# LN0's normalized rows kept in DRAM, and the residual added by VectorE instead of by products with the identity

## The chip, the core and the metric

The kernel runs on one core of a Trainium2 chip. The metric is device time in microseconds for one execution, the median of several runs; lower is better. The core has TensorE (PE, with PEld for its weight loads), VectorE (DVE), ScalarE (ACT), GpSimd (POOL), and SyncE (SP), which here only issues transfers. Sixteen DMA engines move the data of all queues; SP's queue carries the weights, POOL's queue the small tables, gathers and scatters.

## The reference

512 tokens of width 1024 pass one layer of an encoder. The parts that matter here:

```python
h = layer_norm(x, ln0_g, ln0_b)                     # "LN0": rows normalized, then gain and offset
mix = merged @ w_out                                # merged = sigmoid(ga)*out_a + sigmoid(gb)*out_b
h = layer_norm(DN_ALPHA * h + mix, ln1_g, ln1_b)    # the residual h is LN0's output
ffn = routed_experts(h, ...)                        # top 4 of 32 experts per token, chosen by h @ w_router
h = layer_norm(DN_ALPHA * h + ffn, ln2_g, ln2_b)
```

`out_a` and `out_b` are a windowed and a dense attention, each followed by its own branch projection. An expert has three 1024 x 1024 float32 matrices (gate, up, down), 12 MB in all, 32 experts.

## The kernel before

All instructions of an engine run in the order in which the code issues them (a manual schedule), and a tile name with `bufs=n` is a ring of n buffers: the next tile of that name waits until the oldest one's readers are done.

Tokens are four tiles of 128 (t = 0 to 3). At the start `acc` holds x, is normalized in place (mean and variance only), and is transposed; gain and offset go on during the transposition. The result stands as `hTH` + `hTL`, two fp32r parts of LN0's output with the width on the partitions. After that `acc` is used for the attention outputs (`oAB`), which are split into `qs` and `kk` (L702 to L708).

The stretch around the change, in order:

- **Branch projections** (L712 to L728), four rounds `cc`. A round makes four results in PSUM tiles `s` (3 buffers), 12 matmuls each: two for branch A from `qs`, two for branch B from `kk`. VectorE multiplies each by its gate (L721), adds the pairs (L724), and ScalarE and VectorE split the sum, divided by alpha, into two parts `M` (L726, L727). VectorE also makes the low part of the weights that come next (L94).
- **Router constants** (L732 to L744). POOL's queue loads LN1's gain and offset into the ring `P` (4 buffers of 128 x 512, used by the attention until then), then the router's weights `wr` (tile `tab`) and its bias `cb`, then `order` (tile `PT`) and the experts' biases. TensorE multiplies `wr` by LN1's offset (L743), eight products that stand in its order ahead of the output projection.
- **Residual** (L749 to L754). 64 products of 128 x 128 blocks of `hTH` and `hTL` with the identity put LN0's output, turned back to rows, into the eight PSUM tiles `oo` of the output projection.
- **Output projection** `mix` (L756), adding onto them: k = 0 to 3 for all tiles, then k = 4 to 7 tile by tile. After each tile `norm` (L764) takes statistics of the PSUM tiles (L300, L301), and ScalarE writes the normalized rows `z` (L768). Two tiles later `z_turn` transposes them, ScalarE copies the result to `kp` (L779), and `route` (L781) multiplies by `wr` (L784) and picks the four experts. POOL makes h (`affine`, L792) from `z` for the gathers.
- **Order of the experts** (L916 to L958): the counts per expert give `turns` and `turnI`. From expert 1 on SP reads the expert's number from `turnI` (L219) before it can issue a load (L237).

Expert 0's twelve chunks of 1 MB need no number. They are loaded ahead into slots, of which seven are opened at L822 in the space that `hTH`, `hTL`, `kk` and `qs` leave.

Of the kernel before, what the change touches and what calls it, by code (L numbers as in the profile page):

```python
# [10 lines left out]
F32 = mybir.dt.float32  # L11
# [4 lines left out]
AF = mybir.ActivationFunctionType  # L16
OP = mybir.AluOpType
# [4 lines left out]
DM = 1024  # L22
T = 512
NT = T // 128
KT = DM // 128
# [3 lines left out]
ALPHA = 2.0 ** 0.25  # L29
SCALE = HD ** -0.5  # L30
SLOPES = [2.0 ** -(h + 1) for h in range(NH)]
LN_EPS = 1e-5
# [86 lines left out]
def hybrid_attention_moe(ctx: ExitStack, tc: tile.TileContext, x, ln0_g, ln0_b, w_in, a_sink, b_q_norm, b_k_norm,  # L119
                         w_branch_a, w_branch_b, w_out, ln1_g, ln1_b, w_router, b_router, w_gate, b_gate,  # L120
                         w_up, b_up, w_down, b_down, ln2_g, ln2_b, consts, dist, order, rope, out):
    nc = tc.nc
# [6 lines left out]
    def pool(name, **kw):  # L129
        p = tc.alloc_tile_pool(name=name, bufs=1, reuse_waits="tile", **kw)  # L130
        opened.append(p)
        return p

    def close(*pools):
        for p in pools:
            opened.remove(p)
            p.release()

    ctx.callback(lambda: close(*opened[::-1]))
    dram = ctx.enter_context(tc.tile_pool(name="dram", bufs=1, space=DRAM))  # L140
    keep = pool("keep")
    wp = pool("wp")
    hd = pool("hd")
# [16 lines left out]
    def mm3(o, ah, al, bh, bl, start, stop, **kw):  # L160

        for i, (a, b) in enumerate(((ah, bh), (ah, bl), (al, bh))):
            nc.tensor.matmul(o, a, b, start=start and i == 0, stop=stop and i == 2, **kw)  # L163

    def run(g):
        for _ in g:
            pass
# [4 lines left out]
    acc = keep.tile([128, NT, DM], F32, name="acc")  # L172
# [35 lines left out]
    for c in range(4):  # L208
        v = w_out.rearrange("(k p) c -> p k c", p=128)[:, 2 * c:2 * c + 2]
# [80 lines left out]
    def ln_stats(rows_, eps=LN_EPS, pool=keep):  # L290

        return ln_scale(row_stats(rows_, pool), eps, pool)

    def row_stats(rows_, pool=keep):
        n = len(rows_)
        bs = pool.tile([128, n, 2, 6], F32, name="bst", bufs=2 if pool is keep else 1)
        mv = pool.tile([128, n, 2], F32, name="mv", bufs=2 if pool is keep else 1)
        for t, src in enumerate(rows_):
            for i in range(2):
                nc.vector.bn_stats(bs[:, t, i], src[i])  # L300
            nc.vector.bn_aggr(mv[:, t], bs[:, t])  # L301
        return mv

    def ln_scale(mv, eps=LN_EPS, pool=keep):
        n = mv.shape[1]
        r = pool.tile([128, 2, n], F32, name="rstd", bufs=2 if pool is keep else 1)
        rstd_of(r[:, 0], mv[:, :, 1], 1.0, eps)
        nc.vector.scalar_tensor_tensor(r[:, 1], mv[:, :, 0], -1.0, r[:, 0], op0=OP.mult, op1=OP.mult)
        return [(r[:, 0, t:t + 1], r[:, 1, t:t + 1]) for t in range(n)]
# [6 lines left out]
    def two(a):  # L316
        return [a[:, :512], a[:, 512:]]


    hTH = h1.tile([128, KT, T], F32R, name="hTH")  # L320
    hTL = h1.tile([128, KT, T], F32R, name="hTL")
    identr = h1.tile([128, 128], F32R, name="identr")
# [3 lines left out]
    for i in range(2):  # L326
        for t, (r, nmr) in enumerate(stats):
            z = two(acc[:, t])[i]
            if t % 2:
                nc.vector.tensor_scalar(z, z, r, nmr, op0=OP.mult, op1=OP.add)  # L330
            else:
                nc.scalar.activation(z, z, AF.Identity, bias=nmr, scale=r)
    p = ps.tile([128, 32], F32, name="pp", bufs=2)
    nc.tensor.transpose(p, rows, ident[:32, :32])
    nc.vector.tensor_copy(cols, p.rearrange("p (a b) -> p a b", b=8))
# [26 lines left out]
    def proj_k(halves, done, tag, bufs):  # L362
        p = [ps.tile([128, 2, 256], F32, name=tag, bufs=bufs) for _ in range(2)]
        for i, half in enumerate(halves):
            wh, wl = st.get(half)
            for t in (0, 2, 1, 3):
                s = slice(t * 128, t * 128 + 128)
                for k in range(4):
                    q = 4 * i + k
                    o = p[t // 2][:, t % 2]  # L370
                    for j, (a, b) in enumerate(((hTH, wh), (hTL, wh), (hTH, wl))):
                        nc.tensor.matmul(o, a[:, q, s], b[:, k], start=t % 2 == 0 and q == 0 and j == 0,
                                         stop=q == KT - 1 and j == 2, skip_group_check=True)
                if i:
                    done(t, p[t // 2][:, t % 2])
                yield
# [135 lines left out]
    w = {}  # L512
# [27 lines left out]
    bias = [hd.tile([128, T], F32, name=f"gb{h}") for h in range(NH)]  # L540
# [29 lines left out]
    for i in range(2):  # L570
        nc.vector.tensor_tensor(tab[i][:, :, 0], ropes[:, :, 0], qkn[:, i:i + 1].to_broadcast([128, NT, HD]), op=OP.mult)
        for a in range(2):
            sw = qkn[:, i].rearrange("p (h a d) -> p h a d", a=2, d=16)[:, :, 1 - a]
            for t in range(NT):
                nc.vector.tensor_tensor(tab[i][:, t, 1].rearrange("p (h a d) -> p h a d", a=2, d=16)[:, :, a],
                                        ropes[:, t, 1].rearrange("p (h a d) -> p h a d", a=2, d=16)[:, :, a],
                                        sw, op=OP.mult)
# [27 lines left out]
    def q_done(c):  # L605
        def done(t, p):
            s = slice(c * 256, c * 256 + 256)
            nc.scalar.activation(rq[t].rearrange("p n d -> p (n d)")[:, s], p, AF.Copy)
            if c == 0:
                sq[t] = hd.tile([128, T], F32, name="P", bufs=4)  # L610
            nc.scalar.activation(sq[t][:, s], p, AF.Square)
            if c:
                nc.vector.reduce_sum(rs[:, t, 0:8], sq[t].rearrange("p (n d) -> p n d", d=HD), AX.X)
        return done
# [43 lines left out]
    g0, g1 = proj_k(h_bq[0], q_done(0), "s", 3), proj_k(h_bq[1], q_done(1), "pp", 2)  # L658
# [44 lines left out]
    for i, n in enumerate(("qs", "kk")):  # L703
        d = h1.tile([128, 4, DM], F32R, name=n).rearrange("p a (b c) -> p (a b) c", c=T)
# [3 lines left out]
        o_hl.append((d[:, 0:4], d[:, 4:8]))  # L708
    run(gates_b)
    gv = {}  # L710
    M = []
    for cc in range(4):  # L712
        for i, g in enumerate((gA, gB)):
            wh, wl = st.get(h_br[2 * cc + i])
            for c in (2 * cc, 2 * cc + 1):
                nc.scalar.activation(g[c], g[c], AF.Sigmoid)
                p = ps.tile([128, T], F32, name="s", bufs=3)
                s = slice(c % 2 * 128, c % 2 * 128 + 128)
                for k in range(4):
                    mm3(p, wh[:, k, s], wl[:, k, s], o_hl[i][0][:, k], o_hl[i][1][:, k], k == 0, k == 3)  # L720
                nc.vector.tensor_tensor(g[c], p, g[c], op=OP.mult)  # L721
        for c in (2 * cc, 2 * cc + 1):
            m = hd.tile([128, T], F32, name="f", bufs=2)
            nc.vector.tensor_tensor(m, gA[c], gB[c], op=OP.add)  # L724
            h, l = hd.tile([128, T], F32R, name=f"ga{c}"), hd.tile([128, T], F32R, name=f"gb{c}")
            nc.scalar.activation(h, m, AF.Copy, scale=1.0 / ALPHA)  # L726
            nc.vector.scalar_tensor_tensor(l, m, 1.0 / ALPHA, h.bitcast(F32), op0=OP.mult, op1=OP.subtract)  # L727
            M.append((h, l))  # L728

    for n, v in (("g1", ln1_g), ("b1", ln1_b)):  # L732
        for i in range(2):
            gv[n, i] = hd.tile([128, T], F32, name="P", bufs=4)
            nc.gpsimd.dma_start(gv[n, i], v[:, i * 512:i * 512 + 512].to_broadcast([128, 512]))
    wr = hd.tile([128, 2, KT, NE], F32, name="tab")
    nc.gpsimd.dma_start(wr[:, 0], w_router[0].rearrange("(k p) e -> p k e", p=128))
    nc.vector.tensor_tensor(wr[:, 1], wr[:, 0], cols[:, 2][:, :, None].to_broadcast([128, KT, NE]), op=OP.mult)
# [7 lines left out]
    iota_e = con[:, C_IE:C_IE + NE]  # L746
    h1d = dram.tile([T, DM], F32, name="h1d")

    def residual(t, o):  # L749
        s = slice(t * 128, t * 128 + 128)  # L750
        for k in range(KT):
            for h in (hTH, hTL):
                nc.tensor.matmul(o[k // 4][:, k % 4 * 128:k % 4 * 128 + 128], h[:, k, s], identr,
                                 start=k % 4 == 0 and h is hTH, stop=False, skip_group_check=True)  # L754

    def mix(t, o, k, w, last):  # L756
        for i in range(2):
            s = slice(i * 512, i * 512 + 512)
            mm3(o[i], *(m[:, t * 128:t * 128 + 128] for m in M[k]), w[0][:, 0, s], w[1][:, 0, s], False, last,
                skip_group_check=True)  # L760

    z = {}

    def norm(t, o):  # L764
        (r, nmr), = ln_stats([o], LN_EPS / ALPHA ** 2)
        z[t] = [hd.tile([128, T], F32, name=("ga", "gb")[i] + str(t)) for i in range(2)]
        for i in range(2):
            nc.scalar.activation(z[t][i], o[i], AF.Identity, bias=nmr, scale=r)  # L768

    zt = {}  # L770

# [43 lines left out]

    oo = [[ps.tile([128, T], F32, name=n, bufs=b) for _ in range(2)] for n, b in (("pp", 2), ("pt", 2), ("s", 3))]
    oo.append([ps.tile([128, T], F32, name=n, bufs=b) for n, b in (("s", 3), ("o", 1))])
    for t in range(NT):
        residual(t, oo[t])
    close(h1)  # L820
    rp = pool("rp", side="right")
    st.slots(rp, 7)  # L822
# [52 lines left out]
    for k in range(4):  # L875
        w = st.get(h_wo[k])
# [87 lines left out]
    for k in range(KT):  # L964
        f = mp.tile([128, T], F32, name="rT")[:, k % 4 * 128:k % 4 * 128 + 128]
        g, b = (cols1[:, c, k:k + 1] for c in range(2))
        h, l = (d[:, k] for d in XT[0])
# [335 lines left out]
    for e in range(NE):  # L1303
        f = e + 1
        if f < NE:
            gates_of(f, {1: [blocks] if f == 10 else [], 5: [lambda: a_turn(e, 0)], 6: [lambda: a_turn(e, 1)]})
            at = {}
            n = min(2, NE - 3 - f)
# [74 lines left out]
    with tc.If(n_over > 0):  # L1383
# [8 lines left out]
        with tc.For_i(0, n_over, 1) as i:  # L1392
# [31 lines left out]
            def fetch(w):  # L1424
                def get(j):
                    raw = mp.tile([128, DM], F32, name="raw", bufs=3)
                    nc.sync.dma_start(raw, w[0, ds(e, 1)].rearrange("a (p j) f -> (a p) j f", j=8)[:, j])
                    h, l = hl((1, DM))()
                    split_to(h[:, 0], l[:, 0], raw)
                    return h, l  # L1430
                return get
# [12 lines left out]
            o = products(range(8), AT["o"], None, None, "d", {}, fetch(w_down))  # L1444
# [61 lines left out]
```

## Time and profile before

| | us |
|---|---|
| median of 3 runs (1462.32 to 1465.82) | 1463.74 |
| the profiled execution, its own time | 1464.82 |
| its span in the trace, first to last instruction | 1463.0 |

| engine | busy us | share of the span |
|---|---|---|
| PE | 1385.2 | 95% |
| PEld | 925.6 | 63% |
| DVE | 885.3 | 61% |
| ACT | 718.2 | 49% |
| POOL | 226.9 | 16% |

Busy shares are means over stages with different limits, so the page's slices and the windows by stage say more than they do. Times in the rows count from the span's start. In a row of waits, "A <- B" says that A stood idle until B was done.

### The profile page before, as it was taken

The numbers are of one execution on the slowest core, as the hardware profiler recorded it, in microseconds if no ns is written. First come the engines' busy times: TensorE is split into PE (matmuls) and PEld (weight loads), VectorE is DVE, ScalarE is ACT, GpSimd is POOL, SyncE is SP. The second block draws the span as 40 slices with busy tenths as digits, with TensorE's granted clock in tenths as the row PEclk, the third lists the DMA queues.
The fourth block names the chain that finished last, engine by engine and source line by source line (L and its number), as shares of the span: only waits on it lengthen the run. The fifth ranks groups of instructions, "written<-read, shape, count | busy, mean of one in ns | idle before, by whom it ended". The sixth has DMA issues, their size and how long they took to land.

```text
span 1463.0 us, 19181 instructions
## 1 busy us (share of the span) xinstructions
PE 1385.2 (95%) x6837; PEld 925.6 (63%) x6837; DVE 885.3 (61%) x1384; ACT 718.2 (49%) x1016; POOL 226.9 (16%) x264
## 2 busy tenths in 40 slices
PE   5999999999879999999999999999999999999973
PEld 4778977888755547466574755747556486567521
DVE  5666676563674537466584664846547388577355
ACT  5454567533353526355463553735546276566301
POOL 0000200102451110112101121011210103130002
PEclk9999999999889999999999999999999999999987
DMA  6462211327279999999999999999999999999981
GB/s 228 155 230 67 80 37 36 108 94 282 75 260 356 414 423 423 423 399 418 424 422 420 423 423 420 415 415 416 414 417 414 414 408 425 410 409 423 388 365 63
DMA packets 90645, 469.55 MB, mean 321 GB/s; under 512 B 10369, under 2 KB 28977, under 8 KB 42416
## 3 DMA queue, kind: packets, MB, share of 16 engines
q1 hardware_dynamic: 80160, 439.54, 74.0%
q0 software_dynamic: 10384, 28.73, 5.2%
q8 instruction: 55, 0.90, 0.2%
q14 instruction: 46, 0.38, 0.1%
HBM read 451.71 MB, written 24.64 MB: 326 GB/s over the span
## 4 chain that ended last, share of the span: by engine, by line
PE 28%; DMA 22%; issue 17%; DVE 3%; POOL 2%; ACT 1%; POOLq 0%; SPq 0%; DVEq 0%
DMA raw<-in_w_up_dram 6%; DMA raw<-in_w_down_dram 6%; PE d L163 6%; DMA raw<-in_w_gate_dram 6%; PE g L163 5%; PE u L163 5%; PE u L1100 4%; PE g L1100 3%; DMA xg<-h1d,tokI 3%; PE d L1100 3%; POOL hots L801 1%; PE t L1023 1%; DVE raw L1361 1%; PE t L1162 1%; DMA Y<-y,dstI 1%
## 5 line engine op out<-in xcount | busy, mean ns | idle before, releaser
L94 DVE TENSOR_TENSOR wl<-raw,wh 128x1024 fp32r<-128x1024 f32 x428 | 514.8, 1229 | 126.2 <-ACT wh L93 120.2
L93 ACT ACTIVATE wh<-raw 128x1024 fp32r<-128x1024 f32 x428 | 444.8, 1057 | 173.1 <-PE d L163 66.8
L1015 POOL DMA_INDIRECT xg<-h1d,tokI x31 | 46.2, 1491 | 710.3 <-PE t L1162 322.5
L158 DVE TENSOR_TENSOR atl<-t,ath 128x512 fp32r<-128x512 f32 x32 | 22.0, 690 | 153.8 <-ACT ath L157 153.8
L1100 PE MATMUL g<-raw,xth 128*64 128x512 f32 x480 | 112.5, 601 | 0.0
L1100 PE MATMUL d<-raw,ath 128*64 128x512 f32 x480 | 110.4, 599 | 0.0
L1100 PE MATMUL u<-raw,xth 128*64 128x512 f32 x480 | 109.8, 599 | 0.0
L163 PE MATMUL d<-wh,ath 128*128 128x512 f32 x256 | 105.2, 411 | 2.2 <-ACT wh L93 2.2
L163 PE MATMUL d<-wl,ath 128*128 128x512 f32 x256 | 101.8, 398 | 4.8 <-DVE wl L94 4.5
L163 PE MATMUL g<-wh,xth 128*128 128x512 f32 x256 | 103.5, 404 | 0.0
L163 PE MATMUL u<-wh,xth 128*128 128x512 f32 x256 | 102.8, 401 | 0.0
L163 PE MATMUL g<-wh,xtl 128*128 128x512 f32 x256 | 101.5, 397 | 0.5 <-DVE xtl L970 0.5
L163 PE MATMUL u<-wl,xth 128*128 128x512 f32 x256 | 101.9, 398 | 0.0
L163 PE MATMUL u<-wh,xtl 128*128 128x512 f32 x256 | 101.8, 397 | 0.0
L163 PE MATMUL g<-wl,xth 128*128 128x512 f32 x256 | 101.3, 396 | 0.0
L163 PE MATMUL d<-wh,atl 128*128 128x512 f32 x256 | 101.2, 395 | 0.0
L1131 DVE TENSOR_SCALAR u<-u 128x512 f32<-128x512 f32 x48 | 33.4, 696 | 64.0 <-PE u L163 36.8
L1100 PEld LDWEIGHTS u<-raw,xth 128*64 128x64 f32 x480 | 31.7, 136 | 57.7 <-issue 54.2
L1100 PEld LDWEIGHTS d<-raw,ath 128*64 128x64 f32 x480 | 31.6, 136 | 57.3 <-issue 48.5
L163 PE MATMUL pp<-hTH,wh 128*128 128x512 f32 x160 | 63.9, 399 | 0.0
L163 PE MATMUL pp<-hTH,wl 128*128 128x512 f32 x160 | 63.3, 396 | 0.0
L163 PE MATMUL pp<-hTL,wh 128*128 128x512 f32 x160 | 63.2, 395 | 0.0
(423 smaller groups left out, 2304.4 us busy)
## 6 DMA issues: line engine op xcount, KB each, us to landing
raw<-in_w_gate_dram SPq DMA_DIRECT2D x128, 1024.0 KB, 19.7
raw<-in_w_up_dram SPq DMA_DIRECT2D x128, 1024.0 KB, 20.3
raw<-in_w_down_dram SPq DMA_DIRECT2D x128, 1024.0 KB, 21.0
raw<-in_w_in_dram SPq DMA_DIRECT2D x14, 1024.0 KB, 8.9
Y<-u POOLq DMA_DIRECT2D x4, 2048.0 KB, 14.9
raw<-Y SPq DMA_DIRECT2D x8, 1024.0 KB, 16.8
raw<-in_w_out_dram SPq DMA_DIRECT2D x4, 1024.0 KB, 5.0
acc<-in_x_dram SPq DMA_DIRECT2D x4, 512.0 KB, 6.7
```

What stands on the lines that cost most here:

```text
L93: self.nc.scalar.activation(h, src, AF.Copy)
L94: self.low.tensor_tensor(l, src, h.bitcast(F32), op=OP.subtract)
L158: nc.vector.tensor_tensor(l, src, h.bitcast(F32), op=OP.subtract)
L163: nc.tensor.matmul(o, a, b, start=start and i == 0, stop=stop and i == 2, **kw)
L801: eng.tensor_scalar(d[:, t], cnt64 if small else cnt1, places[:, t:t + 1], None, op0=OP.is_equal)
L1015: nc.gpsimd.indirect_dma_start(out=x_[:, :T] if small else x_, out_offset=None, in_=src, in_offset=bass.IndirectOffsetOnAxis(ap=tok, axis= ...
L1023: nc.tensor.transpose(p[:, j], src[:, 4 * i + j::8], ident)
L1100: nc.tensor.matmul(o[64 * i:64 * i + 64], xt(j), w[:, 0, i * 512:i * 512 + 512], start=j == 0 and sel is None, stop=j == 7, skip_group_che ...
L1131: nc.vector.tensor_scalar(u, u, -6.0, 8.0, op0=OP.max, op1=OP.min)
L1162: nc.tensor.transpose(p[:, b], src[:, b:T:4], ident)
L1361: nc.vector.tensor_tensor(two(res[t])[i], two(res[t])[i], two(gb[:, 0])[i], op=OP.mult)
```

## The change

The normalized rows are stored to a DRAM tensor `zd` before `acc` is overwritten (four transfers of 512 KB on POOL's queue). When the attention outputs have been split, LN0's gain and offset are loaded, each as a broadcast of 128 x 512 twice, into the ring `P`, and the rows are loaded back to `acc`. After each round `cc` of the branch projections VectorE applies gain and offset to tile t = cc (`h0_affine`). The 64 products are gone; `mix` starts its PSUM tiles at k = 0, and `norm` adds them to `acc` by VectorE before it takes the statistics.

```diff
+    zd = dram.tile([T, DM], F32, name="zd")
+    for t in range(NT):
+        nc.gpsimd.dma_start(zd[t * 128:t * 128 + 128], acc[:, t])
...
+    def vectors(*nv):
+        for n, v in nv:
+            for i in range(2):
+                gv[n, i] = hd.tile([128, T], F32, name="P", bufs=4)
+                nc.gpsimd.dma_start(gv[n, i], v[:, i * 512:i * 512 + 512].to_broadcast([128, 512]))
+
+    vectors(*((n, v.rearrange("(a d) -> a d", a=1)) for n, v in (("g0", ln0_g), ("b0", ln0_b))))
+    for t in range(NT):
+        nc.gpsimd.dma_start(acc[:, t], zd[t * 128:t * 128 + 128])
+
+    def h0_affine(t):
+        for i in range(2):
+            a = acc[:, t, i * 512:i * 512 + 512]
+            nc.vector.tensor_tensor(a, a, gv["g0", i], op=OP.mult)
+            nc.vector.tensor_tensor(a, a, gv["b0", i], op=OP.add)
...
             M.append((h, l))
-    for n, v in (("g1", ln1_g), ("b1", ln1_b)):
-        for i in range(2):
-            gv[n, i] = hd.tile([128, T], F32, name="P", bufs=4)
-            nc.gpsimd.dma_start(gv[n, i], v[:, i * 512:i * 512 + 512].to_broadcast([128, 512]))
+        h0_affine(cc)
+
+    vectors(("g1", ln1_g), ("b1", ln1_b))
...
-    def residual(t, o):
-        s = slice(t * 128, t * 128 + 128)
-        for k in range(KT):
-            for h in (hTH, hTL):
-                nc.tensor.matmul(o[k // 4][:, k % 4 * 128:k % 4 * 128 + 128], h[:, k, s], identr,
-                                 start=k % 4 == 0 and h is hTH, stop=False, skip_group_check=True)
...
     def mix(t, o, k, w, last):
         for i in range(2):
             s = slice(i * 512, i * 512 + 512)
-            mm3(o[i], *(m[:, t * 128:t * 128 + 128] for m in M[k]), w[0][:, 0, s], w[1][:, 0, s], False, last,
-                skip_group_check=True)
+            mm3(o[i], *(m[:, t * 128:t * 128 + 128] for m in M[k]), w[0][:, 0, s], w[1][:, 0, s], k == 0, last)
...
     def norm(t, o):
-        (r, nmr), = ln_stats([o], LN_EPS / ALPHA ** 2)
+        a = two(acc[:, t])
+        for i in range(2):
+            nc.vector.tensor_tensor(a[i], a[i], o[i], op=OP.add)
+        (r, nmr), = ln_stats([a], LN_EPS / ALPHA ** 2)
...
-            nc.scalar.activation(z[t][i], o[i], AF.Identity, bias=nmr, scale=r)
+            nc.scalar.activation(z[t][i], a[i], AF.Identity, bias=nmr, scale=r)
...
-    for t in range(NT):
-        residual(t, oo[t])
     close(h1)
```

POOL's order from the last small transfers of the attention to the experts' biases, before (`P` is the ring of four, `tab` is `wr`, `PT` is `order`):

```order
L735 DMA P<-in_ln_g_dram 128x512 x2
L735 DMA P<-in_ln_b_dram 128x512 x2
L737 DMA tab<-in_w_router_dram 128x8x32
L740 DMA cb<-in_b_router_dram 128x32
L828 DMA PT<-in_order_dram 128x256
```

and now:

```order
L719 DMA P<-in_ln_g_dram 128x512 x2
L719 DMA P<-in_ln_b_dram 128x512 x2
L724 DMA acc<-zd 128x1024 x4
L719 DMA P<-in_ln_g_dram 128x512 x2
L719 DMA P<-in_ln_b_dram 128x512 x2
L756 DMA tab<-in_w_router_dram 128x8x32
L759 DMA cb<-in_b_router_dram 128x32
L840 DMA PT<-in_order_dram 128x256
```

The first two pairs are now LN0's; LN1's come as the second use of the ring, and `wr` and all that follows stand behind them.

TensorE's order at the end of the branch projections and the start of the output projection, before:

```order
L163 MATMUL s<-kk,wh 128x512 x2
L163 MATMUL s<-kk,wl 128x512
L743 MATMUL o<-tab,cols 128x32 x8
L753 MATMUL pp<-identr,hTH 128x128
L753 MATMUL pp<-identr,hTL 128x128
```

and now:

```order
L163 MATMUL s<-kk,wh 128x512 x2
L163 MATMUL s<-kk,wl 128x512
L762 MATMUL o<-tab,cols 128x32 x8
L163 MATMUL pp<-wh,ga_2958 128x512
L163 MATMUL pp<-wl,ga_2958 128x512
L163 MATMUL pp<-wh,gb_2959 128x512
```

The products with `wr` (now L762) keep their place, and the output projection follows them directly.

VectorE's order from the end of round 1 of the branch projections into round 2, now (before, L729 and L730 are not there, and L742 is L721):

```order
L745 TENSOR_TENSOR f<-ga_785,gb_2449 128x512
L748 SCALAR_TENSOR_TENSOR gb_3051<-f,ga_3050 128x512
L729 TENSOR_TENSOR acc<-acc,P 128x512
L730 TENSOR_TENSOR acc<-acc,P 128x512
L729 TENSOR_TENSOR acc<-acc,P 128x512
L730 TENSOR_TENSOR acc<-acc,P 128x512
L94 TENSOR_TENSOR wl<-raw_1_2509,wh 128x1024
L742 TENSOR_TENSOR ga_900<-s,ga_900 128x512
L742 TENSOR_TENSOR ga_1013<-s,ga_1013 128x512
```

The four operations of `h0_affine` stand between the end of a round and the operations that free the next round's first PSUM tiles; after the last round they stand directly ahead of what uses `wr`.

## Rows read from the trace of the kernel before

**Rows 1.** The page's 40 slices of the span: busy tenths.
```profile
PE   5999999999879999999999999999999999999973
DMA  6462211327279999999999999999999999999981
```

**Rows 2.** Waits of SP's queue: total us, times, longest us.
```profile
SPq L219 <- DVE turns L958: 20.7, 1, 20.7
SPq L237 <- PE o L753: 13.4, 1, 13.4
```

**Rows 3.** Windows: busy us of PE, PEld, DVE, ACT, POOL, then PEclk, DMA share, GB/s.
```profile
400.00:450.00 50.00, 39.22 (x185) 27.25 (x184) 32.59 (x82) 21.77 (x29) 19.95 (x22) 0.90 0.67 241
450.00:500.00 50.00, 50.00 (x232) 24.60 (x232) 21.22 (x28) 20.17 (x25) 10.97 (x13) 1.00 1.01 418
```

**Rows 4.** Timeline of PE around the residual: start us, us, instruction.
```profile
316.61 1.86 PE L743 MATMUL o<-tab,cols 128*128 128x32 f32 x16
...
318.31 0.31 PE L753 MATMUL pp<-identr,hTH 128*128 128x128 f32 x1
...
325.37 0.28 PE L753 MATMUL o<-identr,hTL 128*128 128x128 f32 x1
325.49 0.45 PE L163 MATMUL pp<-wh,ga 128*128 128x512 f32 x1
```

**Rows 5.** VectorE's operations in the branch projections, grouped by line: busy us, mean ns.
```profile
L724 DVE TENSOR_TENSOR f<-ga,gb 128x512 f32<-128x512 f32 x8 | 5.5, 684 | 0.0
```

**Rows 6.** Timeline of VectorE from round 0 into round 1, and round 3's end.
```profile
287.25 0.69 DVE L727 SCALAR_TENSOR_TENSOR gb<-f,ga 128x512 fp32r<-128x512 f32 x1 [0.70 <-ACT ga L726]
288.21 1.23 DVE L94 TENSOR_TENSOR wl<-raw,wh 128x1024 fp32r<-128x1024 f32 x1 [0.26 <-ACT wh L93]
289.35 1.28 DVE L721 TENSOR_TENSOR ga<-s,ga 128x512 f32<-128x512 f32 x2
...
320.86 0.69 DVE L727 SCALAR_TENSOR_TENSOR gb<-f,ga 128x512 fp32r<-128x512 f32 x1 [0.70 <-ACT ga L726]
```

**Rows 7.** Timeline of PE: the eighth of the branch projections' 16 results begins.
```profile
291.40 0.40 PE L163 MATMUL s<-kk,wh 128*128 128x512 f32 x1
```

**Rows 8.** Timeline of POOL: issues of LN1's offset, the router's weights and bias.
```profile
256.87 1.16 POOL L735 DMA_DIRECT2D P<-in_ln_b_dram  x2 [2.32 <-PE pt L453]
258.01 0.90 POOL L737 DMA_DIRECT2D tab<-in_w_router_dram  x1
258.91 0.55 POOL L740 DMA_DIRECT2D cb<-in_b_router_dram  x1
```

**Rows 9.** Transfers of POOL's queue: issues, KB each, median us from issue to landing.
```profile
xg<-h1d,tokI POOLq DMA_INDIRECT x31, 8.4
...
PT<-in_order_dram POOLq DMA_DIRECT2D x1, 128.0 KB, 4.0
...
bd<-in_b_down_dram POOLq DMA_DIRECT2D x1, 128.0 KB, 7.5
...
cb<-in_b_router_dram POOLq DMA_DIRECT2D x1, 16.0 KB, 4.6
```

**Rows 10.** Timeline of SP's queue: expert 0's first load, then the next two.
```profile
311.86 0.37 SPq L237 DMA_DIRECT2D raw<-in_w_gate_dram  x1
...
325.57 0.88 SPq L237 DMA_DIRECT2D raw<-in_w_gate_dram  x2
```

**Rows 11.** Windows around a stop of PE after 404 us; columns as in rows 3.
```profile
404.00:406.00 2.00, 0.00 (x0) 0.00 (x0) 1.53 (x5) 1.04 (x3) 0.00 (x0) 1.00 1.01 426
410.00:412.00 2.00, 2.00 (x9) 1.55 (x9) 1.09 (x4) 0.62 (x2) 1.13 (x2) 0.50 1.00 414
412.00:414.00 2.00, 2.00 (x11) 1.45 (x9) 1.05 (x1) 1.39 (x2) 2.00 (x4) 0.76 0.28 115
```

**Rows 12.** Timeline of PE: the router's products for tiles 0 and 1.
```profile
364.45 1.97 PE L784 MATMUL pp<-tab,kp 128*128 128x32 f32 x16 [0.37 <-ACT kp L779]
...
374.49 2.82 PE L784 MATMUL pp<-tab,kp 128*128 128x32 f32 x16 [1.43 <-ACT kp L779]
```

## The prediction, made before the changed kernel ran

> **What bounds the kernel now.** I read the page's slices first. The reader should see the DMA engines at 9 in every slice but the last two from the thirteenth on, with TensorE at 9 beside them [rows 1]: from about 450 us the experts' weights, 384 MB, run at the rate the engines have, 418 GB/s at a share of 1.01 [rows 3]. So the end moves with the moment at which this stream starts, and not with work done under it. The waits of SP's queue, second, say what starts it: SP stood 20.7 us until `turns` was there [rows 2], the experts' order, the last link of a chain through branch projections, output projection, norm, router and counts. Expert 0's loads need no order and were long in. Between 400 and 450 us the DMA share is only 0.67 and TensorE is busy 39 of 50 us [rows 3]; there the kernel waits for expert 0's own chain (transposes, tables, gathers), which starts from the same `turns`. So I take a shift of `turns` at one for one at the end. The third view is the timeline of TensorE, VectorE and POOL between 256 and 400 us, for that is where the change lies.
>
> **What is removed.** The 64 products with the identity run from 318.31 us, and the output projection begins at 325.49 [rows 4]: 7.2 us on the chain. Without them it could begin at 318.3. The wait of 13.4 us by which SP held expert 0's loads for the residual's tiles [rows 2] goes too. That alone is worth nothing, since SP afterwards waits for `turns` anyway; but it moves up to 8 MB of weights ahead, into the stretch in which the new small loads run.
>
> **VectorE in the branch projections.** `h0_affine` is four operations of 128 x 512 a round. Such an addition takes 684 ns [rows 5]; two of the four can start 0.6 us after the one ahead, so 2.66 us. They start when L727 ends at 287.94; L94, which had waited 0.26 us for ScalarE, then begins at 290.6 and the first L721 follows 1.14 us later and ends at 292.4 instead of 290.0 [rows 6]. It frees the PSUM buffer that TensorE takes for its eighth result at 291.40 [rows 7] (three buffers, so the eighth needs the fifth's). TensorE is held 1.0 us there, and at the next two rounds alike: **+3.0 us**. If VectorE overlaps more than I think it is 0; the 1.4 us of room in these rows keeps it under 4.
>
> **The router's weights.** This is the term that decides. Before, `wr` was issued at 258.01 [rows 8], 58 us before TensorE wants it at 316.61 [rows 4]. Now LN1's four loads take the ring `P` a second time, and the last two must wait for the last additions of `h0_affine(3)`; `wr` stands behind them on POOL, and on TensorE the eight products with `wr` stand ahead of the whole output projection. Step by step: L727 of the last round ended at 321.55 [rows 6], now 324.55; four operations, 327.2. The first two loads are issued at 325.2 and 326.5, when their multiplications are done, the other two follow at 0.58 each (1.16 for two [rows 8]), so POOL reaches `wr` at 328.2. From issue to landing the trace shows no time for `wr`. The nearest rows: 128 KB alone in the queue 4.0 us, the bias `cb` 0.9 us behind `wr` 4.6 us (so `wr` took at most 5.5, if they are served in order), 128 KB on this queue amid weights 7.5, a gather amid weights 8.4 [rows 9]. Expert 0's loads, the first of which went out at 311.86 and the next at 325.57 [rows 10], will now go out from about 316 to 322, since three slots lie on `hTH` and `hTL`, which nobody reads any more; 8 MB at 418 GB/s fill the engines until 336. So I take the loaded row of the same size, 7.5: `wr` lands at 335.7, its products take 1.86 [rows 4], and the output projection begins at 337.6 instead of 325.49: **+12.1 us** in all so far, the removed 7.2 and the 3.0 already in it. With 4.0 us it would be +8.6; if the small loads are served only after the 8 MB, 1.2 MB at some 290 GB/s behind 336, `wr` lands at 340 and it is +16.4.
>
> The Trainium skill, "DMA: Bandwidth & Descriptors", section "Anatomy of one DMA — SWDGE (gpsimd) path", gives a fit for such a transfer of 2.0 us and the bytes over 436 GB/s, an estimate of 2.3 us for 128 KB. The sum would then be 5.2 us lower. The rows disagree, with 4.0 us for as many bytes alone [rows 9]; and the same page, section "SWDGE vs HWDGE vs iDMA", says that each DMA engine goes round between the queues, which speaks for a price that grows when weights are under way, as 7.5 against 4.0 does here.
>
> **TensorE's clock.** It stands still from about 319.6 to 335.7. After a stop the granted clock falls: idle in 404 to 406, it is at 0.50 (1.2 GHz) in 410 to 412 and at 0.76 in 412 to 414 [rows 11], so some 4 us at half speed after it starts again: **+2.0 us**, between 1 and 3.3.
>
> **Norm.** Each tile now needs two additions before its statistics, 1.3 us. This shows twice in the middle, where the router's products already waited 0.37 and 1.43 us for `kp` [rows 12], a copy that stands behind the norm's `z` on ScalarE: both waits grow by 1.3 and the rest of the output projection is behind them. At the last tile 0.7 of the 1.3 remains, the rest under transposes and `pick`. **+3.3 us**; at least 1.3 (the last tile alone), at most 5.2 (four tiles).
>
> **Costed at nothing.** Storing `zd` (2 MB near 20 us) and loading it back (2 MB near 265 to 275 us) fall into slices in which the DMA engines are at 6 and 3 [rows 1]; without that cover each would cost 5 us. The stores stand on POOL ahead of a table that is not needed for tens of microseconds. `acc` is back well before 288, when `h0_affine(0)` wants it.
>
> **The sum.** 12.1 + 2.0 + 3.3 = +17.4 us. The profiled execution took 1464.82 us (1.8 outside its span), so it would take 1482.2; it lies 1.1 above the median of the runs, so I predict **1481.0 us** (rounded), 1.2% slower.
>
> **Rivals.** *The wait is short.* No stall in the loop, `wr` in 4.0 us, the clock's loss 1.0, the norm 1.3: POOL reaches `wr` at 325.2, it lands at 329.2, the projection starts at 331.1, +5.6, in all +7.9 or 1471.6. For it: alone in the queue these loads did take 4.0. Against it: the weights are moved into the very stretch.
>
> *The small loads come last.* +16.4, clock 3, norm 4: +23.4, 1487.1. For it: `wr` has rows of 128 bytes, many more pieces than the other loads.
>
> *Faster.* TensorE is not held at L762 at all: if the second use of `P` got its buffers before the rounds are over, `wr` would be there as now, 7.2 would come off, 0 to 3.0 go on in the loop and 1.3 to 3.3 in the norm, from -0.9 to -5.9: about 1460. It decides as soon as `wr` lands before 319. Against it: two of the four buffers hold LN0's offset until the last additions, which end at 324.2 even without a stall; nothing lets POOL pass.
>
> *Absorbed.* The late `turns` is caught up between 400 and 450, where the DMA share is 0.67 [rows 3]: about 1464. Against it: what is slow there hangs on `turns` too.
>
> **Chances.** Forecast, +12 to +21 (1476 to 1485): 0.55. Short wait: 0.20. Loads last: 0.16. Absorbed or another mix that ends level: 0.05. Faster: 0.04. A measurement of this kernel tells about 0.2% from no change, so faster 0.04, within it 0.04, slower 0.92. The range takes in most of the short and the long wait, 1470 to 1488.
>
> **What would show it.** In the changed kernel's timeline TensorE should stand some 16 us ahead of L762, released by the DMA to `tab`; POOL should issue L756 near 328; three gaps of 1 us should stand at the start of the later rounds; the waits for `kp` should be near 1.7 and 2.8 us; SP's wait for `turns` should grow. I am wrong in the sign if TensorE goes from the branch projections into the output projection without a gap, and in the size if `wr` lands much outside 332 to 340 or if the end does not follow `turns`.

## The result, and the profile after

The changed kernel takes 1487.78 us (1487.21 to 1489.55, 4 runs) against 1464.24 for the kernel before (4 runs): a ratio of 1.0155, interval 1.013 to 1.018. It is slower by 23.5 us and 6.8 us above the predicted 1481.0; it lies in the range that was given, 1470 to 1488, by 0.2 us at its upper end. Its profiled execution took 1487.59 us, with a span of 1485.7.

What TensorE waits for between the branch projections and expert 0, in the changed kernel (engine, tile, line, releaser: us in total, times, longest):

```profile
PE o L762 <- DMA tab<-in_w_router_dram: 19.1, 1, 19.1
...
PE pp L798 <- ACT kp L793: 4.3, 2, 2.6
...
PE s L163 <- DVE ga L742: 2.5, 3, 0.8
```

The first of them was not there before. TensorE's timeline at that place (start us, us; in brackets the idle time ahead and its releaser) answers to [rows 4]:

```profile
319.41 0.40 PE L163 MATMUL s<-kk,wl 128*128 128x512 f32 x1
338.87 3.59 PE L762 MATMUL o<-tab,cols 128*128 128x32 f32 x16 [19.06 <-DMA tab<-in_w_router_dram]
342.27 0.77 PE L163 MATMUL pp<-wh,ga 128*128 128x512 f32 x1
```

The branch projections end 3.0 us later, TensorE stands for 19 us in front of the sixteen instructions of L762, these take 3.59 us instead of 1.86, and the output projection begins at 342.27 instead of 325.49. POOL's timeline, which answers to [rows 8]:

```profile
325.47 0.54 POOL L719 DMA_DIRECT2D P<-in_ln_g_dram  x1 [53.96 <-DVE acc L729]
326.38 0.54 POOL L719 DMA_DIRECT2D P<-in_ln_g_dram  x1 [0.37 <-issue]
326.92 1.15 POOL L719 DMA_DIRECT2D P<-in_ln_b_dram  x2
328.05 0.90 POOL L756 DMA_DIRECT2D tab<-in_w_router_dram  x1
```

POOL stood 54 us until VectorE's multiplications had freed the ring, and reached the router's weights at 328.05; before, they went out at 258.01. The transfers issued between 316 and 345 us (KB each, median us from issue to landing), which answer to [rows 9]:

```profile
P<-in_ln_g_dram POOLq DMA_DIRECT2D x2, 256.0 KB, 7.8
P<-in_ln_b_dram POOLq DMA_DIRECT2D x2, 256.0 KB, 9.5
tab<-in_w_router_dram POOLq DMA_DIRECT2D x1, 128.0 KB, 10.7
```

Each lands later after its issue than the one ahead of it. SP's timeline shows what is under way beside them, as in [rows 10], and the first loads that need an expert's number:

```profile
316.11 2.34 SPq L237 DMA_DIRECT2D raw<-in_w_gate_dram  x4
319.83 2.74 SPq L237 DMA_DIRECT2D raw<-in_w_up_dram  x4
...
421.96 2.43 SPq L237 DMA_DIRECT2D raw<-in_w_gate_dram  x4
```

Eight loads of 1 MB are issued by 322.6 us. VectorE's copy of `turns`, in the kernel before and then in the changed one:

```profile
399.32 0.17 DVE L958 COPY turns<-pp 128x32 f32<-128x32 f32 x1
```

```profile
420.42 0.17 DVE L970 COPY turns<-pp 128x32 f32<-128x32 f32 x1
```

It is 21.1 us late, and the span is 22.7 us longer.

### The profile page after: what moved, and what is told of

The parts are those of the page before. It is cut to its first block, busy times and chain, and to the rows that moved or that the text cites. A ratio compares the mean times of both kernels' runs of the same rounds, so it can differ in the third digit from the quotient of the medians.

```text
span 1485.7 us, 19104 instructions
## 1 busy us (share of the span) xinstructions
PE 1385.6 (93%) x6773; PEld 923.0 (62%) x6773; DVE 898.7 (60%) x1408; ACT 718.5 (48%) x1016; POOL 231.8 (16%) x276
## 4 chain that ended last, share of the span: by engine, by line
PE 40%; DMA 15%; issue 11%; DVE 3%; POOL 1%; ACT 1%; SPq 0%; POOLq 0%; ACTq 0%; DVEq 0%
PE d L163 8%; PE g L163 7%; PE u L163 7%; PE g L1112 5%; PE u L1112 5%; DMA raw<-in_w_up_dram 5%; DMA raw<-in_w_gate_dram 5%; DMA raw<-in_w_down_dram 4%; PE d L1112 4%; PE t L1035 1%; DMA xg<-h1d,tokI 1%; POOL hots L815 1%; PE t L1174 1%; DVE wl L94 1%; DVE raw L1373 1%
```

## The experiments

The ratios are to the kernel before, whose time beside them on the same chip was 1464.66 us (first four) or 1465.85 us (last three).

**The router's tables ahead of LN1's loads.** One thing is undone.

```diff
-    vectors(("g1", ln1_g), ("b1", ln1_b))
     wr = hd.tile([128, 2, KT, NE], F32, name="tab")
...
         nc.gpsimd.dma_start(raws[i], (b_gate, b_up)[i // 2][0][:, i % 2 * T:i % 2 * T + T])
+
+    vectors(("g1", ln1_g), ("b1", ln1_b))
```

> The changed kernel with one thing undone: LN1's gain and offset are loaded behind the router's weights, bias, order and the experts' biases instead of ahead of them, so the router's weights no longer stand behind the ring P. Theory A (the wait for the router's weights at L762, 19.1 us, and the half clock behind it are nearly the whole loss): the eight products run at once at 319.6 us, the output projection starts near 321.4 instead of 342.3, and 2.5 us of half clock go too, so 1487.8 - 20.9 - 2.5 = about 1464 us, level with the kernel before (what the removed products give, 7.2, is used up by 3.0 in the branch projections, about 2 in the norm and 1.6 later). Rival B (the additions in norm and the new traffic carry a large part): 1475 us or more.

Measured: 1464.32 us, ratio 0.9999 (0.9989 to 1.0009). TensorE's timeline:

```profile
319.72 1.87 PE L761 MATMUL o<-tab,cols 128*128 128x32 f32 x16
321.42 0.48 PE L163 MATMUL pp<-wh,ga 128*128 128x512 f32 x1
...
327.81 0.50 PE L163 MATMUL o<-wh,ga 128*128 128x512 f32 x1 [1.31 <-DVE cb L762]
```

There is no wait for the router's weights and no half clock behind them, and all 23.5 us are gone. The loss is the late load, not the change of the residual as such, and rival B falls. One short wait is left: for the fourth tile TensorE needs the PSUM tile `o`, which VectorE reads for `cb` (L762 in this run) only after the additions of `h0_affine(3)`. So the 7.2 us that the 64 products gave are used up by 3.0 in the branch projections, by this 1.3, and by some 2.5 in the norm.

**The affine moved out of the branch projections.** On top of the edit before:

```diff
             M.append((h, l))
-        h0_affine(cc)
...
-    vectors(("g1", ln1_g), ("b1", ln1_b))
...
         w = st.get(h_wo[k])
         biases(k)
+        h0_affine(k)
         for t in range(NT):
             mix(t, oo[t], k, w, False)
+    vectors(("g1", ln1_g), ("b1", ln1_b))
```

> As the run before, and h0_affine(k) moved out of the branch projections into the first half of the output projection (one tile per k = 0 to 3), with LN1's loads behind it. Theory A: the three holds of TensorE in the branch projections, 0.8 us each by the trace, go; the output projection starts near 318.4, 2.5 to 3.0 us earlier than in the run before: about 1461 us, 2 to 4 us under the kernel before. Rival: VectorE is now late with the low parts of the weights (L94) in the output projection, TensorE waits there instead, and it is no better than the run before, 1464 us or more.

Measured: 1461.76 us, ratio 0.9977 (0.9968 to 0.9987): faster than both kernels. The three waits for L742 are not in its list of waits any more, and neither is the 1.3 us for `cb`: `turns` comes 4.0 us earlier than in the run before (395.07 against 399.10). TensorE's timeline, and VectorE's copy of `turns`:

```profile
316.94 1.87 PE L760 MATMUL o<-tab,cols 128*128 128x32 f32 x16
318.65 0.48 PE L163 MATMUL pp<-wh,ga 128*128 128x512 f32 x1
```

```profile
395.07 0.17 DVE L970 COPY turns<-pp 128x32 f32<-128x32 f32 x1
```

The output projection starts 6.8 us earlier than before the change, nearly all that the 64 products took; `turns` comes 4.2 us earlier. The difference of 2.6 us is lost between the two, where `norm` now has its additions.

**Expert 0's weights held back.** In the changed kernel:

```diff
+    for h in (hTH, hTL):
+        nc.tensor.matmul(oo[0][0][:, :128], h[:, 0, :128], identr, start=True, stop=True)
     close(h1)
```

> The changed kernel with two small products that read hTH and hTL, put directly behind the products with the router's weights, so that all but one of expert 0's loads wait for them. Only what lies beside the small loads changes. Theory A (the router's weights took 10.7 us because the experts' weights were under way): they land in about 5.5 us, near 333.6, the wait at L762 falls from 19.1 to about 14, and the time to about 1482.6 us. Rival B (they are slow of their own, by their short rows and the four loads ahead of them in the queue): landing 10 us or more, 1488 us.

Measured: 1481.9 us, ratio 1.011 (1.0093 to 1.0126). The landing of the router's weights, and TensorE's wait:

```profile
tab<-in_w_router_dram POOLq DMA_DIRECT2D x1, 128.0 KB, 4.4
```

```profile
333.04 3.59 PE L762 MATMUL o<-tab,cols 128*128 128x32 f32 x16 [12.74 <-DMA tab<-in_w_router_dram]
```

With the same four loads ahead of it but without the weights beside it, the load takes 4.4 us instead of 10.7, and 5.9 us of the time come back. Theory A holds, and more than it said.

**TensorE kept busy through the wait.** In the changed kernel, products whose results nobody reads:

```diff
+    d = ps.tile([128, T], F32, name="pp", bufs=2)
+    for k in range(76):
+        nc.tensor.matmul(d, M[0][0][:, :128], M[0][0], start=True, stop=True)
     p = ps.tile([128, NE], F32, name="o")
     for k in range(KT):
         nc.tensor.matmul(p, cols[:, 3, k:k + 1].to_broadcast([128, 128]), wr[:, 0, k], start=k == 0, stop=k == KT - 1)
```

> The changed kernel with 76 products without use (one part of M times itself, 128x512) on TensorE between the branch projections and L762, 17.8 us of work in a wait of 19.1 us. Theory A (the stop costs a half clock on top of the wait: 1.5 us in L762 and 2.5 us in the output projection): L762 takes 1.9 us, the output projection starts 1.5 us earlier and runs at full clock, 1483.8 us. Rival B (the clock costs nothing here, since other work sets the pace): 1488 us. If the products last longer than the wait, L762 is late by the difference.

Measured: 1482.87 us, ratio 1.0121 (1.0105 to 1.0136), 4.9 us under the changed kernel. TensorE's timeline at the end of the wait (L765 is L762), and windows from there (busy us of PE, PEld, DVE, ACT, POOL, then PEclk, DMA share, GB/s):

```profile
338.16 1.94 PE L765 MATMUL o<-tab,cols 128*128 128x32 f32 x16 [1.29 <-DMA tab<-in_w_router_dram]
339.94 0.48 PE L163 MATMUL pp<-wh,ga 128*128 128x512 f32 x1
```

```profile
338.00:340.00 2.00, 1.84 (x17) 1.87 (x17) 0.42 (x1) 0.00 (x0) 0.00 (x0) 1.00 1.05 299
340.00:342.00 2.00, 2.00 (x7) 1.62 (x7) 1.86 (x7) 0.63 (x1) 0.00 (x0) 0.64 1.02 336
342.00:344.00 2.00, 2.00 (x6) 1.52 (x6) 0.73 (x2) 0.00 (x0) 0.00 (x0) 0.50 1.02 408
344.00:346.00 2.00, 2.00 (x11) 1.63 (x10) 0.00 (x0) 0.00 (x0) 0.00 (x0) 1.00 1.05 436
```

L765 takes 1.94 us at full clock instead of 3.59. The half clock in the output projection became shorter but did not go: it came a little later, behind the 1.29 us for which TensorE still stood. So theory A has the time, but not the full clock. The output projection starts 2.3 us earlier, 0.7 of it because the load went out and landed a little earlier here; its first twelve matmuls take 4.4 us instead of 5.3; `turns` comes 2.4 us earlier. So the clock has a price behind the wait. The 4.9 us of the time are more than `turns` shows, and where the rest arises behind it these runs do not show.

**Rows stored and loaded, unused.** In the kernel before, with the residual still made by products:

```diff
+    zd = dram.tile([T, DM], F32, name="zd")
+    for t in range(NT):
+        nc.gpsimd.dma_start(zd[t * 128:t * 128 + 128], acc[:, t])
...
     gv = {}
+    for t in range(NT):
+        nc.gpsimd.dma_start(acc[:, t], zd[t * 128:t * 128 + 128])
```

> The kernel before with one part of the change alone: the normalized rows are stored and loaded back to acc, where nobody uses them; the residual is still made by the 64 products. Theory A (the traffic of 4 MB is under cover, as the prediction has it): no change, within 1.5 us of the kernel before. Rival B (it disturbs the first weights or the small loads of POOL's queue, up to 5 us each way): 1467 to 1475 us.

Measured: 1463.85 us, ratio 0.9991 (0.9974 to 1.0008). The 4 MB cost nothing that can be measured.

**The additions in norm made twice**, in the version with the affine moved:

```diff
+        z[t] = [hd.tile([128, T], F32, name=("ga", "gb")[i] + str(t)) for i in range(2)]
+        for i in range(2):
+            nc.vector.tensor_tensor(z[t][i], a[i], o[i], op=OP.add)
         for i in range(2):
             nc.vector.tensor_tensor(a[i], a[i], o[i], op=OP.add)
         (r, nmr), = ln_stats([a], LN_EPS / ALPHA ** 2)
-        z[t] = [hd.tile([128, T], F32, name=("ga", "gb")[i] + str(t)) for i in range(2)]
```

> The version with the router's tables first and the affine later (e2_affine_later, 1461.8 us), with the two additions in norm made twice for each tile, the first time into a tile that is then overwritten. The price of the additions is read from the step. Theory A (each tile's additions stand on the chain as the prediction says, 3.3 us for the four; the trace of the changed kernel gives 1.8 to 2.6): 1464 to 1465 us, and the waits for kp grow to about 2.9 and 5.2 us. Rival B (they are covered by the transposes and picks): 1462 us.

Measured: 1464.53 us, ratio 0.9989 (0.9976 to 1.0002). The two ratios differ by 0.0012, or 1.8 us, with intervals that overlap; the spans of the two profiled executions differ by 3.0 (1462.2 and 1459.2), and `turns` comes 4.6 us later. So the additions stand on the chain, at 1.8 (by the ratios) to 4.6 us (by `turns`) for the four tiles; a closer price these runs do not give. The waits for `kp`:

```profile
360.05 3.62 PE L798 MATMUL pp<-tab,kp 128*128 128x32 f32 x16 [2.86 <-ACT kp L793]
374.25 1.97 PE L798 MATMUL pp<-tab,kp 128*128 128x32 f32 x16 [1.25 <-ACT kp L793]
```

The first grew as was expected, from the 1.66 us of the version with the affine moved to 2.86; the second did not (2.63 there). Behind the longer first wait the same products took 3.62 us instead of 1.97, with the clock at 0.50 from 360 to 368 us, and TensorE came later to the second tile. Part of the 4.6 us is therefore clock.

**The router's weights under the same weights, but first in the queue.** In the changed kernel:

```diff
-                gv[n, i] = hd.tile([128, T], F32, name="P", bufs=4)
+                gv[n, i] = hd.tile([128, T], F32, name="tab") if (n, i) == ("b1", 1) else hd.tile([128, T], F32, name="P", bufs=4)
...
-    vectors(("g1", ln1_g), ("b1", ln1_b))
-    wr = hd.tile([128, 2, KT, NE], F32, name="tab")
+    wr = hd.tile([128, T], F32, name="P", bufs=4).rearrange("p (a k e) -> p a k e", a=2, k=KT)
...
     nc.gpsimd.dma_start(cb, b_router.to_broadcast([128, NE]))
+    vectors(("g1", ln1_g), ("b1", ln1_b))
```

> The changed kernel with the router's weights in the first buffer of the ring P that comes free and LN1's four loads behind them (LN1's last piece in the tile that the router's weights had). They are issued near 325.5 us, under the same stream of expert 0's weights, but with nothing ahead of them in POOL's queue. It tells why they took 10.7 us in the changed kernel and not the 7.5 of the prediction. Theory Q (place in the queue, behind four loads of 256 KB): landing in 7.5 us or less, at about 333; L762 then starts 5.9 us earlier than at 338.9, and the time is about 1482 us. Theory S (their own short rows amid the weights): landing 10 us or more after the issue, at about 336, 1485 us.

Measured: 1483.27 us, ratio 1.0107 (1.008 to 1.0134). The transfers:

```profile
tab<-in_ln_b_dram POOLq DMA_DIRECT2D x1, 256.0 KB, 12.8
P<-in_w_router_dram POOLq DMA_DIRECT2D x1, 128.0 KB, 7.0
```

```profile
333.16 3.59 PE L762 MATMUL o<-P,cols 128*128 128x32 f32 x16 [12.84 <-DMA P<-in_w_router_dram]
```

The load itself takes 7.0 us under the weights when nothing is ahead of it, and LN1's last piece, now behind it, takes 12.8; L762 starts 5.7 us earlier than in the changed kernel. Theory Q holds by the landing (the time alone, between 1482 and 1485, would not tell). Three numbers for the same 128 KB: 4.4 us behind four loads without weights, 7.0 amid weights and first, 10.7 amid weights and behind four loads.

## Why the prediction was right, and where its size was off

| step | predicted | measured, changed kernel |
|---|---|---|
| branch projections end later | +3.0 | +3.0 (319.41 against 316.37 in TensorE's timeline) |
| POOL issues the router's weights | 328.2 | 328.05 |
| they land after | 7.5 | 10.7 |
| wait in front of L762 | some 16 | 19.1 |
| output projection begins | 337.6 | 342.27 |
| half clock, L762 and after | 2.0 | 1.7 + 2.5 |
| norm | 3.3 | 1.9 (what is left at `turns`) |
| later than `turns` | 0 | 1.6 |
| in the profiled executions | +17.4 | +22.8 |

Of the 6.8 us between the predicted and the measured time, 5.4 are the difference in the last line: about 3.2 for the landing, 2.2 for the clock and 1.6 behind `turns`, less 1.4 for the norm. The rest is the step from the profiled execution to the median, for which 1.2 was taken off.

**The mechanism was right.** The 7.2 us that the products took do come back when nothing else is late, as the version with the affine moved shows. They were lost by a transfer that the diff hardly touches: LN1's vectors take the ring `P` a second time, the router's weights stand behind them on POOL, and TensorE wants them ahead of the output projection. That undoing this order alone returns the whole loss settles it.

**The held branch projections.** VectorE's timeline answers to [rows 6] almost to the tenth; TensorE's, to [rows 7]:

```profile
287.02 0.69 DVE L748 SCALAR_TENSOR_TENSOR gb<-f,ga 128x512 fp32r<-128x512 f32 x1 [0.70 <-ACT ga L747]
287.63 0.68 DVE L729 TENSOR_TENSOR acc<-acc,P 128x512 f32<-128x512 f32 x1
288.34 0.69 DVE L730 TENSOR_TENSOR acc<-acc,P 128x512 f32<-128x512 f32 x1
288.95 0.69 DVE L729 TENSOR_TENSOR acc<-acc,P 128x512 f32<-128x512 f32 x1
...
290.28 1.22 DVE L94 TENSOR_TENSOR wl<-raw,wh 128x1024 fp32r<-128x1024 f32 x1
291.42 1.28 DVE L742 TENSOR_TENSOR ga<-s,ga 128x512 f32<-128x512 f32 x2
```

```profile
292.16 0.73 PE L163 MATMUL s<-kk,wh 128*128 128x512 f32 x2 [0.83 <-DVE ga L742]
```

**The step that was mis-sized** is the landing of the router's weights: "So I take the loaded row of the same size, 7.5". They took 10.7, 3.2 us more, and the wait in front of L762 grew with it. In the kernel before, the load of that row had one scatter ahead of it in its queue:

```profile
496.98 1.62 POOL L1144 DMA_INDIRECT Y<-y,dstI  x1 [1.16 <-ACT y L1143]
498.60 0.58 POOL L1194 DMA_DIRECT2D bd<-in_b_down_dram  x1
```

The router's weights had four loads of 256 KB ahead of them, which the prediction used for the moment of issue and did not count again for the transfer; with nothing ahead, amid weights, they took 7.0. The row of 4.0 us, which the prediction calls alone in the queue, was not alone either: `order` went out 1.7 us behind the router's weights and 0.8 behind the bias [rows 8].

```profile
259.72 0.54 POOL L828 DMA_DIRECT2D PT<-in_order_dram  x1 [0.27 <-issue]
```

What it lacked was the experts' weights beside it; without these the four loads ahead cost little too, as the 4.4 us show.

The rival in which the small loads come last has nearly the measured time (1487.1), and its landing, 340, lies 1.2 us from the 338.8 measured. That is luck: it has them served only after the 8 MB, which it has at an end by 336.

```profile
raw<-in_w_up_dram SPq DMA_DIRECT2D x4, 1024.0 KB, 22.6
```

These loads were issued from 319.8 us on, so by their median at least two of them landed after 342, when the router's weights had been there for 3 us. The small loads were under way beside the weights, and not behind them.

The fit of the Trainium skill ("DMA: Bandwidth & Descriptors", section "Anatomy of one DMA — SWDGE (gpsimd) path"), an estimate of 2.3 us, is under all three measured landings. What the Trainium skill says in section "SWDGE vs HWDGE vs iDMA" of the same page, that each DMA engine goes round between the queues, agrees with 4.4 against 10.7 us, and with a load of the router's weights that lands before the last of the experts' weights issued ahead of it.

**The clock** cost twice what was put down. Windows of the changed kernel, as in [rows 11]:

```profile
338.00:340.00 2.00, 1.14 (x6) 1.17 (x6) 0.43 (x1) 0.00 (x0) 0.00 (x0) 0.50 1.02 292
342.00:344.00 2.00, 2.00 (x7) 1.71 (x7) 1.50 (x7) 0.00 (x0) 0.00 (x0) 0.50 1.03 375
346.00:348.00 2.00, 2.00 (x7) 1.57 (x6) 0.00 (x0) 0.00 (x0) 0.00 (x0) 0.57 0.88 362
348.00:350.00 2.00, 2.00 (x11) 1.62 (x10) 0.00 (x0) 0.00 (x0) 0.00 (x0) 1.00 0.24 98
```

It is at 0.50 (1.2 GHz) from the restart at 338.9 to about 347.5, some 8.6 us and not 4. L762 loses 1.7 us (3.59 against 1.86). The output projection's thirteenth matmul, in the kernel before and then in the changed one:

```profile
328.30 0.39 PE L163 MATMUL s<-wh,ga 128*128 128x512 f32 x1
```

```profile
347.54 0.47 PE L163 MATMUL s<-wh,ga 128*128 128x512 f32 x1
```

The twelve ahead of it take 5.27 us instead of 2.81, and lose 2.5. In the last experiment, with a wait of 12.8 us, the half clock lasted 8.7 us. Why it lasted about twice as long as the prediction read from [rows 11] was not tried.

**Norm** cost less: the waits for `kp` came as predicted, which answers to [rows 12],

```profile
385.06 1.97 PE L798 MATMUL pp<-tab,kp 128*128 128x32 f32 x16 [1.65 <-ACT kp L793]
...
396.29 1.97 PE L798 MATMUL pp<-tab,kp 128*128 128x32 f32 x16 [2.62 <-ACT kp L793]
```

but of the 21.1 us at `turns` the start of the projection has 16.8 and the clock behind it 2.5 (21.10, 16.78 and 2.46), which leaves 1.9. The same subtraction gives 2.6 in the version with the affine moved, and 2.5 in the one before it without its wait for `cb`. These remainders hold every other shift of the clock as well: before, half clock fell on the second of these products (2.82 us in [rows 12]), and now it does not. So the price of the additions alone is not known better than that.

**What did not come as said.** SP's wait for `turns` did not grow (20.0 us against the 20.7 of [rows 2]): SP issues the last of expert 0's loads near 400.6 us instead of 378.8, since that load stands until `route` has run (30.5 us, against 28.1 before), so that SP arrives at `turns` later as well. And the end follows `turns` only roughly, by 1.6 us more here; in the seven experiments the span moved between 1.3 us less and 3.0 us more than `turns`. What makes these few us between 420 us and the end was not tried and stays open.

## What to carry to other kernels

Moving a buffer ring's second use behind new readers delays everything that stands behind it on the same queue: follow the queue to the first load that an engine needs in order, and put that load ahead. Price such a load by what is beside it and by what is ahead of it in its queue, both times for the transfer and not only for the issue. And a wait on TensorE is to be booked with the slow clock behind it, in the instruction that waited as well (here 4.2 us behind 19.1).

## What the runs showed of the hardware

The clock fell after a short stop in one run and not in another. In the run with TensorE kept busy, after 17 us of products without a gap, TensorE stood 1.29 us, started again at 1.00 with the sixteen instructions of the router's products, and was at 0.50 in the window from 342 to 344 us, when it had been busy again for 4 us. With the router's tables first it stood 1.31 us between matmuls of the output projection, and the clock was at 1.00 in every window of 2 us from 326 to 336. What tells the two apart was not tried. With the stop of 19.1 us it was already at 0.50 when work came back.

Two neighbouring VectorE operations of 128 x 512 that do not depend on each other start 0.61 us apart although each shows 0.69; one that needs the result of the one ahead starts 0.71 us after it (288.34 to 288.95, and 287.63 to 288.34 us, in the changed kernel).
